# RG-LRU layer on one core: half-angle root, convolution split as a step of its own, weights split one block ahead, input gate's product beside the gates

## The chip, the cores and the metric

The kernel runs on one core of a Trainium2 chip. The metric is the device time of one execution in microseconds (us). Five engines work side by side, each through its own queue in order: TensorE (PE, with its weight loads as PEld), VectorE (DVE), ScalarE (ACT), GpSimd (POOL) and SyncE (SP), which here issues all DMA transfers.

## The reference

One inference step of two layers over 128 context tokens and 1024 latent tokens, 1024 channels each. The first layer (gated linear recurrence and neighbourhood attention) is not touched. The second layer is this:

```python
def odd_mixer(h, w_in, w_out, conv_w, conv_b, gate_w, gate_b, lam, s0):
    xb, g = jnp.split(h @ w_in, 2, axis=-1)
    xc = centred_dwconv(xb, conv_w, conv_b).astype(jnp.float32)
    ...
    for d in range(2):
        gates = jnp.einsum('bthi,ghij->gbthj', xblk, gate_w[d]...) + gate_b[d]
        r = jax.nn.sigmoid(gates[0])
        i = jax.nn.sigmoid(gates[1])
        log_a = -RG_C * r * jax.nn.softplus(-lam[d])
        a = jnp.exp(log_a)
        u = jnp.sqrt(-jnp.expm1(2.0 * log_a)) * (i * xc)
        hs, h_fin = linear_recurrence(a, u, s0[:, d])   # h[t] = a[t] * h[t-1] + u[t]; d = 1 runs backwards
    y = (outs[0] + outs[1]) * jax.nn.silu(g)
    return y @ w_out, ...
```

`RG_C` is 8, and the gate weights are eight blocks of 128 x 128 for each direction and gate. All of it is in float32.

## The kernel before

**Layout.** In the second layer channels lie on the 128 partitions and the 1152 tokens along the free dimension, in three chunks of 384. The eight groups of 128 channels are called j (0 to 7). float32 products on PE are made of three products: each operand is split into a rounded high half and the remainder, and high x high, high x low and low x high are summed in PSUM. The high half is an ACT copy (`wh`, `hTh`, `xch`, `yh`), the low half a subtraction on POOL or DVE (`wl`, `hTl`, `xcl`, `yl`).

**Input projection.** The 16 weight blocks of `w_in` are worked off in the order `ORD1` (0, 1, 2, 3, 8, 4, 9, 5, 10, 6, 11, 7, 12 to 15; blocks 0 to 7 give `xb` of one j, blocks 8 to 15 its gate path `g`), three units of 24 matmuls each (one per chunk), so 48 positions `pos`. `xb_unit` (L1143) writes its result from PSUM with ACT into the padded tile `xp`; `g_unit` (L1162) makes `sg` with ACT and DVE (L1171). Both begin with `w_get(i, 3, 3)`: load weight block i + 3 (tile `wraw`) and split up to i + 3 into `wh` and `wl` (L186).

**Per j, hung on positions.** `conv_all` (L1180) loads and splits the gate weights (`gw`) and runs `conv` (L1055): four DVE instructions over 1155 columns into `xc` (L1059, L1061), two ACT copies into `xch` and two DVE subtractions into `xcl` (L1067). `rg_front` (L1173) runs `gates` for both directions (per direction six groups of three matmuls into PSUM tags a and b, each taken out by an ACT tanh: the recurrence gate into `gr`, the input gate into `yT` or `gi`), then `rg_exp` twice: ACT tanh into `rt`, ACT exp in place in `gr`, which is then a; a squared into `ra` (on POOL for d = 0, L1112, on ACT for d = 1); and `rt = (a*a + 1) * rt` on DVE (L1113). `rg_root` is two ACT square roots, which need another function table than tanh and exp (L74 is the load of a table). `rg_back` runs `rg_scan` for both directions: input gate plus one times `xc` on DVE (four pieces, L1126), times the root on POOL (three chunks, L1128), the scan on DVE in four pieces (L1137), and for d = 1 the sum of both directions (L1142). `y_fin` multiplies by `sg` (L1177). The lists `PC`, `PF`, `PS`, `PK`, `PY` give the positions of convolution, front, root, back and end for each j.

**Output projection.** `w_split(.., V)` at the positions `WP` splits the eight blocks of `w_out`, with the low halves on DVE; `out_tiles` (L994 to L996) multiplies nine token tiles, the first two in an order that takes channel groups 6 and 7 last. `y_split` makes `yh` and `yl` (L977).

**What sets the order.** A scheduler turns the program into one queue for each engine. The order as written is a priority: an instruction whose inputs and buffers are ready by the scheduler's reckoning passes earlier ones that are not, and on the chip each queue then runs strictly in that order. Nearly all tiles of this layer wider than 512 columns, and the weights, come from one pool of 20 buffers (`slab`); a tile that finds none free waits for one, and so does the DMA that fills it. PSUM has three buffers of tag mm, one of o (both for the units) and two each of a and b.

Of the kernel before, what the change touches and what calls it, by code (L numbers as in the profile page):

```python
# [11 lines left out]
AF = mybir.ActivationFunctionType  # L12
OP = mybir.AluOpType
# [3 lines left out]
T = 1152  # L17
NCH = 3
CW = 384
# [14 lines left out]
def trunk_kernel(ctx: ExitStack, tc: tile.TileContext, x, wm0, wm, bmr, wfe, wv, woe, wfo, woo, rgw, sm, st0,  # L34
# [7 lines left out]
    V, A, G, PE = nc.vector, nc.scalar, nc.gpsimd, nc.tensor  # L42
# [4 lines left out]
    def slab(name, shape=(128, T), dt=F32):  # L47
        return sp.tile(list(shape), dt, name=name, tag="slab")
# [58 lines left out]
    def smc(n, i=None, j=None):  # L107
        a, b = SM[n]
        if i is None:
            return smt[:, a:b]  # L110
        return smt[:, a + i:a + (i + 1 if j is None else j)]
# [39 lines left out]
    V.tensor_scalar(sp_t[3], sp_t[3], 2.0, None, OP.mult)  # L151
    V.tensor_scalar(sp_t[0], sp_t[0], 0.0, None, OP.max)
    V.tensor_tensor(sp_t[3], sp_t[3], sp_t[0], OP.add)
    V.tensor_scalar(rgc, sp_t[3], 4.0, None, OP.mult)
    V.tensor_scalar(nrgc, sp_t[3], -4.0, None, OP.mult)
    V.tensor_scalar(hgb, smc("gateb"), 0.5, None, OP.mult)

# [38 lines left out]
    def w_get(i, la_load, la_split):  # L196
        w_split(i)
        w_split(i + la_split)
        w_load(i + la_load)
        return split[i]  # L200
# [845 lines left out]
        gw[h] = (hi, lo)  # L1046

    XP, XC, XS, GR, GI, RH = {}, {}, {}, {}, {}, {}

    def xc_of(j, a, b):  # L1050

        o = 0 if b <= 128 else 3
        return XC[j][:, a + o:b + o]

    def conv(j):  # L1055
        xp = XP.pop(j)
        acc = slab("xc", (128, 1155))
        w = [smc("convw", 4 * j + i) for i in range(4)]
        V.tensor_scalar(acc, xp[:, 0:1155], w[0], smc("convb", j), OP.mult, OP.add)  # L1059
        for i in (1, 2, 3):  # L1060
            V.scalar_tensor_tensor(acc, xp[:, i:i + 1155], w[i], acc, op0=OP.mult, op1=OP.add)  # L1061
        hi, lo = slab("xch", dt=F32R), slab("xcl", dt=F32R)
        XC[j], XS[j] = acc, (hi, lo)
        for a, b in ((0, 128), (128, T)):
            act(hi[:, a:b], xc_of(j, a, b), AF.Copy)
        for a, b in ((0, 128), (128, T)):
            V.tensor_tensor(lo[:, a:b], xc_of(j, a, b), hi[:, a:b].bitcast(F32), OP.subtract)  # L1067

    def gates(j, d):

        hi, lo = XS[j]
        wh, wl = gw[j]
        GR[j, d] = slab("gr")
        dst = [mini("yT") for c in range(3)] if d == 0 or j < 6 else None
        if d == 0:
            for c in range(3):
                yT[j, c] = dst[c]
        else:
            if dst is None:
                gi = slab("gi")  # L1080
                dst = [gi[:, c * CW:(c + 1) * CW] for c in range(3)]
            GI[j] = dst
        for c in range(3):
            z = slice(c * CW, (c + 1) * CW)
            for q in range(2):
                g = 2 * d + q
                ps = psum(("a", "b")[q])
                o = ps[:, :CW]
                n = slice(g * 128, (g + 1) * 128)
                PE.matmul(o, wh[:, n], hi[:, z], start=True, stop=False)  # L1090
                PE.matmul(o, wh[:, n], lo[:, z], start=False, stop=False)
                PE.matmul(o, wl[:, n], hi[:, z], start=False, stop=True)
                i = (d * 2 + q) * 8 + j
                act(GR[j, d][:, z] if q == 0 else dst[c], o, AF.Tanh, scale=0.5, bias=hgb[:, i:i + 1])
        if d == 1:
            XS.pop(j)
            gw.pop(j)

    RT = {}

    def rg_exp(j, d):

        r = GR[j, d]
        t = RT[j, d] = slab("rt")
        ci = slice(d * 8 + j, d * 8 + j + 1)
        act(t, r, AF.Tanh, scale=rgc[:, ci], bias=rgc[:, ci])
        act(r, r, AF.Exp, scale=nrgc[:, ci], bias=nrgc[:, ci])
        t2 = slab("ra")
        if d:
            act(t2, r, AF.Square)  # L1110
        else:
            G.tensor_tensor(t2, r, r, OP.mult)  # L1112
        V.scalar_tensor_tensor(t, t2, 1.0, t, op0=OP.add, op1=OP.mult)  # L1113

    def rg_sqrt(j, d):
        act(RT[j, d], RT[j, d], AF.Sqrt, scale=0.25)
# [1 line left out]
    def rg_scan(j, d):  # L1118
        a, r = GR.pop((j, d)), RT.pop((j, d))
        ci = d * 8 + j  # L1120
        s0c = smc("s0", ci)
        us = [yT[j, c] for c in range(3)] if d == 0 else GI.pop(j)
        segs = ((0, 0, 128), (0, 128, CW), (1, CW, 2 * CW), (2, 2 * CW, T))
        for c, x0, x1 in segs:
            u = us[c][:, x0 - c * CW:x1 - c * CW]
            V.scalar_tensor_tensor(u, u, 1.0, xc_of(j, x0, x1), op0=OP.add, op1=OP.mult)  # L1126
        for c in range(3):
            G.tensor_tensor(us[c], us[c], r[:, c * CW:(c + 1) * CW], OP.mult)  # L1128
        prev = {0: 0.0, 128: s0c} if d == 0 else {128: 0.0, T: s0c}
        for c, x0, x1 in segs[::-1] if d else segs:  # L1130
            u, av = us[c][:, x0 - c * CW:x1 - c * CW], a[:, x0:x1]
            st = prev.get(x1 if d else x0)
            if st is None:
                st = us[c + 1][:, 0:1] if d else us[c - 1][:, CW - 1:CW]
            if d:
                u, av = u[:, ::-1], av[:, ::-1]
            V.tensor_tensor_scan(u, av, u, st, OP.mult, OP.add)  # L1137
        V.tensor_copy(rgfin[:, ci:ci + 1], us[0][:, 0:1] if d else us[0][:, 127:128])
        if d:
            XC.pop(j)  # L1140
            for c in range(3):
                V.tensor_tensor(yT[j, c], yT[j, c], us[c], OP.add)  # L1142

# [2 lines left out]
    def xb_unit(j, c):  # L1146
        if j not in XP:
            XP[j] = slab("xp", (128, SLAB))
            V.memset(XP[j][:, 0:2], 0.0)
            V.memset(XP[j][:, 130:133], 0.0)  # L1150
            V.memset(XP[j][:, 1157:1158], 0.0)
        w_get(POS1[j], 3, 3)
        o = unit_f(POS1[j], c)
        if c == 0:
            act(XP[j][:, 2:130], o[:, 0:128], AF.Copy)
            act(XP[j][:, 133:389], o[:, 128:CW], AF.Copy)
        else:
            act(XP[j][:, 5 + c * CW:5 + (c + 1) * CW], o, AF.Copy)
        if c == 2:
            split.pop(POS1[j])  # L1160
# [1 line left out]
    SG = {}  # L1162

    def g_unit(j, c):
        w_get(POS1[8 + j], 3, 3)
        if j not in SG:
            SG[j] = slab("sg")
        o = unit_f(POS1[8 + j], c)
        sg = SG[j][:, c * CW:(c + 1) * CW]
        act(sg, o, AF.Tanh, scale=0.5)  # L1170
        V.scalar_tensor_tensor(sg, sg, 1.0, o, op0=OP.add, op1=OP.mult)  # L1171
        if c == 2:
            split.pop(POS1[8 + j])  # L1173
# [32 lines left out]
    ends = {n: i + 1 for i, (n, c) in enumerate(seq)}  # L1206
    ev = {}
    for j in range(8):
        for p, f in ((max(ends[j], PC[j]), conv_all), (PF[j], rg_front), (PS[j], rg_root), (max(PK[j], PS[j]), rg_back),
                     (max(PK[j] + 1, PS[j] + 1, ends[8 + j], PY[j]), y_fin)):  # L1210
            ev.setdefault(p, []).append((f, j))

# [5 lines left out]
    for pos in range(max(ev) + 1):  # L1218
# [6 lines left out]
        n, c = seq[pos]  # L1225
# [147 lines left out]
```

## Time and profile before

| | us |
|---|---|
| median of 3 runs (range) | 1283.1 (1281.62 to 1284.45) |
| the profiled execution | 1288.07 |
| its span, first to last instruction | 1286.1 |
| PE busy in the span | 1207.2 (94%) |
| DVE busy | 685.7 (53%) |
| ACT busy | 540.1 (42%) |
| POOL busy | 381.2 (30%) |

The profiled execution lies 5.0 us over the median, and 2.0 us of it lie outside the span. Matmuls are pipelined: one lasts about 340 ns in the records while they begin some 175 ns apart, so a busy PE says only that it wasn't standing. The second layer's mixer runs from about 904 us to 1184 us of the span, the output projection behind it until about 1280 us. A row of a timeline gives start, duration, engine, line, output and inputs, and in brackets how long the engine stood before it and what ended that.

### The profile page before, as it was taken

The page shows a single profiled execution, that of the slowest core. Times are in us where ns is not written, and L with a number is a line of the kernel's source. Part 1 is how long each engine was busy: PE and PEld are TensorE (multiplying, and loading weights), DVE is VectorE, ACT ScalarE, POOL GpSimd, SP SyncE. Part 2 cuts the span into 40 slices and gives each one's busy share as a digit, 9 for nine tenths or more (in the row PEclk, how much of TensorE's full clock was granted, in tenths as well). Part 3 has the DMA queues.
Part 4 walks back from the last instruction along what each step waited for, and adds up shares of the span by engine and source line. Part 5 has one row for each costly group of instructions (what it writes and reads, how often), then busy time and mean ns, then how long its engine had stood idle before and what let it go on. Part 6 is the DMA issues. An engine that isn't in the chain of part 4 may idle for free.

```text
span 1286.1 us, 19174 instructions
## 1 busy us (share of the span) xinstructions
PE 1207.2 (94%) x7536; PEld 1083.1 (84%) x7536; DVE 685.7 (53%) x1422; ACT 540.1 (42%) x1065; POOL 381.2 (30%) x271
## 2 busy tenths in 40 slices
PE   4999998999999999998999999999989899988997
PEld 3889998999999997887866667888988789987886
DVE  5547128315455200000267896644678978799844
ACT  3435134324342211111246774314467576676311
POOL 0143032420515110201250420117355564644000
PEclk8999999999998999998969999999989999999999
DMA  9410100111011455523320325223001101112432
GB/s 355 186 34 21 34 17 26 40 48 37 22 35 36 156 172 189 205 87 108 128 99 17 100 83 181 81 98 131 17 26 42 42 25 42 41 33 95 137 129 82
DMA packets 41909, 110.45 MB, mean 86 GB/s; under 512 B 4180, under 2 KB 14804, under 8 KB 41820
## 3 DMA queue, kind: packets, MB, share of 16 engines
q1 hardware_dynamic: 41820, 109.24, 25.2%
q8 instruction: 59, 0.97, 0.3%
q14 instruction: 30, 0.25, 0.1%
HBM read 96.61 MB, written 12.61 MB: 85 GB/s over the span
## 4 chain that ended last, share of the span: by engine, by line
PE 52%; DVE 14%; ACT 6%; issue 4%; DMA 4%; POOL 2%; SPq 1%; POOLq 0%; ACTq 0%; DVEq 0%
PE ps_mm L316 7%; PE ps_mm L318 7%; PE ps_mm L317 7%; PE ps_mm L995 5%; PE ps_mm L996 5%; PE ps_mm L994 5%; DMA wraw<-in_wfe_dram 3%; DVE yT L1137 2%; DVE xc L1061 2%; DVE P L857 2%; ACT P L77 1%; PE ps_a L221 1%; PE ps_mm L339 1%; PE ps_mm L341 1%; PE ps_mm L340 1%
## 5 line engine op out<-in xcount | busy, mean ns | idle before, releaser
L316 PE MATMUL ps_mm<-hTh,wh 128*128 128x384 f32 x936 | 321.2, 347 | 14.6 <-ACT xp L77 4.8
L317 PE MATMUL ps_mm<-hTl,wh 128*128 128x384 f32 x936 | 320.3, 343 | 2.3 <-DVE hTl L307 1.7
L318 PE MATMUL ps_mm<-hTh,wl 128*128 128x384 f32 x936 | 319.8, 342 | 1.1 <-POOL wl L186 1.1
L186 POOL TENSOR_TENSOR wl<-wraw,wh 128x1024 fp32r<-128x1024 f32 x50 | 127.5, 2552 | 284.3 <-ACT wh L77 254.6
L316 PEld LDWEIGHTS ps_mm<-hTh,wh 128*128 128x128 f32 x936 | 178.1, 191 | 31.1 <-ACT kq L77 7.4
L317 PEld LDWEIGHTS ps_mm<-hTl,wh 128*128 128x128 f32 x936 | 178.8, 191 | 4.6 <-DVE hTl L307 3.3
L318 PEld LDWEIGHTS ps_mm<-hTh,wl 128*128 128x128 f32 x936 | 178.7, 191 | 1.9 <-POOL wl L186 1.7
L995 PE MATMUL ps_mm<-wl,yh 128*128 128x512 f32 (+1 forms) x288 | 113.6, 395 | 4.6 <-DVE wl L186 4.6
L996 PE MATMUL ps_mm<-wh,yl 128*128 128x512 f32 (+1 forms) x288 | 112.6, 391 | 0.0
L994 PE MATMUL ps_mm<-wh,yh 128*128 128x512 f32 (+1 forms) x288 | 112.4, 392 | 0.0
L77 ACT ACTIVATE wh<-wraw 128x1024 fp32r<-128x1024 f32 x68 | 71.3, 1058 | 70.5 <-DMA wraw<-in_wfe_dram 40.6
L262 POOL TENSOR_TENSOR ss<-ss,nhalf 128x1 f32<-128x1 f32 x27 | 15.2, 564 | 243.4 <-DVE ss L261 186.2
L339 PE MATMUL ps_mm<-wh,hTh 128*128 128x256 f32 x288 | 83.2, 289 | 2.1 <-ACT va L77 2.1
L341 PE MATMUL ps_mm<-wh,hTl 128*128 128x256 f32 x288 | 82.0, 285 | 0.0
L340 PE MATMUL ps_mm<-wl,hTh 128*128 128x256 f32 x288 | 81.7, 284 | 0.0
L77 ACT ACTIVATE res<-xt 128x512 f32<-128x512 f32 (+1 forms) x37 | 23.0, 621 | 123.6 <-DVE xt L1004 115.7
L995 PEld LDWEIGHTS ps_mm<-wl,yh 128*128 128x128 f32 x288 | 54.5, 189 | 19.4 <-DVE wl L186 7.7
L822 POOL TENSOR_TENSOR nbm<-mkt,bT 128x384 f32<-128x384 f32 x42 | 45.5, 1103 | 85.2 <-DVE nm L868 40.4
L365 DVE SCALAR_TENSOR_TENSOR yT<-yT,ps_mm 128x384 f32<-128x384 f32 x10 | 5.5, 554 | 113.6 <-ACT yT L77 113.6
L994 PEld LDWEIGHTS ps_mm<-wh,yh 128*128 128x128 f32 x288 | 54.4, 189 | 12.3 <-issue 0.3
L996 PEld LDWEIGHTS ps_mm<-wh,yl 128*128 128x128 f32 x288 | 54.6, 189 | 11.4
L1128 POOL TENSOR_TENSOR yT<-yT,rt 128x384 f32<-128x384 f32 x42 | 56.4, 1371 | 23.4 <-ACT rt L77 19.3
(260 smaller groups left out, 2501.1 us busy)
## 6 DMA issues: line engine op xcount, KB each, us to landing
wm<-in_wm_dram SPq DMA_DIRECT2D x48, 512.0 KB
wraw<-in_wfe_dram SPq DMA_DIRECT2D x28, 512.0 KB
xt<-in_x_dram SPq DMA_DIRECT2D x18, 512.0 KB
bT<-in_bias_dram SPq DMA_DIRECT2D x48, 192.0 KB
wraw<-in_wfo_dram SPq DMA_DIRECT2D x16, 512.0 KB
x_d<-xt SPq DMA_DIRECT2D x9, 512.0 KB
xt<-x_d SPq DMA_DIRECT2D x9, 512.0 KB
out_dram<-xt SPq DMA_DIRECT2D x18, 256.0 KB
```

What stands on the lines that cost most here:

```text
L77: i = A.activation(out, in_, func, **kw)
L186: (lo_eng or G).tensor_tensor(lo, r, hi.bitcast(F32), OP.subtract)
L316: PE.matmul(o, w1, hh, start=(k == 0), stop=False)
L317: PE.matmul(o, w1, hl, start=False, stop=False)
L318: PE.matmul(o, w2, hh, start=False, stop=(k == 7))
L339: PE.matmul(o, hh, w1, start=(k == 0), stop=False)
L340: PE.matmul(o, hh, w2, start=False, stop=False)
L341: PE.matmul(o, hl, w1, start=False, stop=(k == 7))
L994: PE.matmul(o[:, :q - p], yh[:, z], wh[:, p:q], start=(k == 0), stop=False)
L995: PE.matmul(o[:, :q - p], yh[:, z], wl[:, p:q], start=False, stop=False)
L996: PE.matmul(o[:, :q - p], yl[:, z], wh[:, p:q], start=False, stop=(k == 7))
L1128: G.tensor_tensor(us[c], us[c], r[:, c * CW:(c + 1) * CW], OP.mult)
```

## The change

- `rg_exp` ends after tanh and exp. The constant `rgc` is halved, so the tanh is taken at half the angle; with x = -log a, tanh(x/2) = (1 - a)/(1 + a), and the square root of it times (1 + a) is the root of 1 - a*a. The factor is applied behind the root, by a DVE instruction at the head of `rg_scan`.
- The two ACT copies and two DVE subtractions of the split of `xc` leave `conv` for `conv_split`, hung two positions later.
- `w_get` in both units splits one block ahead; loads stay three ahead.
- The product (input gate + 1) * `xc` moves from `rg_scan` to the end of `gates`, and `xc` is given up there.

```diff
-    V.tensor_scalar(rgc, sp_t[3], 4.0, None, OP.mult)
+    V.tensor_scalar(rgc, sp_t[3], 2.0, None, OP.mult)
...
+        XC[j] = acc
+
+    def conv_split(j):
         hi, lo = slab("xch", dt=F32R), slab("xcl", dt=F32R)
-        XC[j], XS[j] = acc, (hi, lo)
+        XS[j] = (hi, lo)
...
+        for c, x0, x1 in SEGS:
+            u = dst[c][:, x0 - c * CW:x1 - c * CW]
+            V.scalar_tensor_tensor(u, u, 1.0, xc_of(j, x0, x1), op0=OP.add, op1=OP.mult)
         if d == 1:
             XS.pop(j)
+            XC.pop(j)
...
-        t2 = slab("ra")
-        if d:
-            act(t2, r, AF.Square)
-        else:
-            G.tensor_tensor(t2, r, r, OP.mult)
-        V.scalar_tensor_tensor(t, t2, 1.0, t, op0=OP.add, op1=OP.mult)
...
+        V.scalar_tensor_tensor(r, a, 1.0, r, op0=OP.add, op1=OP.mult)
         us = [yT[j, c] for c in range(3)] if d == 0 else GI.pop(j)
-        segs = ((0, 0, 128), (0, 128, CW), (1, CW, 2 * CW), (2, 2 * CW, T))
-        for c, x0, x1 in segs:
-            u = us[c][:, x0 - c * CW:x1 - c * CW]
-            V.scalar_tensor_tensor(u, u, 1.0, xc_of(j, x0, x1), op0=OP.add, op1=OP.mult)
...
-        w_get(POS1[j], 3, 3)
+        w_get(POS1[j], 3, 1)
...
-        w_get(POS1[8 + j], 3, 3)
+        w_get(POS1[8 + j], 3, 1)
...
-        for p, f in ((max(ends[j], PC[j]), conv_all), (PF[j], rg_front), ...
+        for p, f in ((max(ends[j], PC[j]), conv_all), (max(ends[j], PC[j]) + 2, conv_split), (PF[j], rg_front), ...
```

## Rows read from the trace of the kernel before

**Rows 1.** The page's slices (40 equal ones; busy share of TensorE in tenths).
```profile
PE   4999998999999999998999999999989899988997
```
**Rows 2.** Waits of PE, 860 us on, for DVE: total us, times, longest.
```profile
PE ps_mm L995 <- DVE wl L186: 4.1, 4, 2.0
```
**Rows 3.** Timeline of PE: the five matmuls that ended its long waits for ACT.
```profile
958.08 0.69 PE L316 MATMUL ps_mm<-hTh,wh 128*128 128x384 f32 x1 [4.79 <-ACT xp L77]
...
994.46 0.45 PE L1090 MATMUL ps_a<-xch,gw 128*128 128x384 f32 x1 [2.03 <-ACT gr L77]
...
1026.43 0.69 PE L1090 MATMUL ps_b<-xch,gw 128*128 128x384 f32 x1 [6.16 <-ACT yT L77]
...
1061.25 0.45 PE L1090 MATMUL ps_a<-xch,gw 128*128 128x384 f32 x1 [3.22 <-ACT gr L77]
...
1130.63 0.69 PE L1090 MATMUL ps_a<-xch,gw 128*128 128x384 f32 x1 [3.51 <-ACT gr L77]
```
**Rows 4.** Stretches: length, busy us (instructions) of PE, PEld, DVE, ACT, POOL, PEclk.
```profile
956.20:962.80 6.60, 4.72 (x15) 4.72 (x16) 6.60 (x16) 4.83 (x10) 2.45 (x1) 0.50 0.01 2
963.00:969.80 6.80, 6.80 (x39) 6.45 (x39) 5.49 (x9) 4.86 (x7) 0.70 (x2) 1.00 0.26 77
...
904.00:1184.00 280.00, 254.75 (x1378) 246.01 (x1376) 230.65 (x300) 191.29 (x270) 143.53 (x81) 0.96 0.13 40
```
**Rows 5.** Timeline of ACT: two of the copies `xch` and their waits.
```profile
956.33 1.26 ACT L77 ACTIVATE xch<-xc 128x128 fp32r<-128x128 f32 x2 [5.05 <-DVE xc L1061]
...
1023.45 1.26 ACT L77 ACTIVATE xch<-xc 128x128 fp32r<-128x128 f32 x2 [11.32 <-DVE xc L1061]
```
**Rows 6.** Waits of DVE and of ACT, 904 to 1190 us.
```profile
DVE rt L1113 <- POOL ra L1112: 23.5, 6, 9.4
...
ACT xch L77 <- DVE xc L1061: 38.5, 7, 11.3
```
**Rows 7.** Timeline of DVE: L1113 and what came ahead of the convolutions.
```profile
940.46 1.36 DVE L1113 SCALAR_TENSOR_TENSOR rt<-ra,rt 128x1152 f32<-128x1152 f32 x1 [9.39 <-POOL ra L1112]
943.39 1.36 DVE L1113 SCALAR_TENSOR_TENSOR rt<-ra,rt 128x1152 f32<-128x1152 f32 x1 [1.56 <-ACT ra L77]
944.66 1.59 DVE L1059 TENSOR_SCALAR xc<-xp,smt 128x1155 f32<-128x1155 f32 x1
...
971.69 1.36 DVE L1113 SCALAR_TENSOR_TENSOR rt<-ra,rt 128x1152 f32<-128x1152 f32 x1 [3.20 <-POOL ra L1112]
...
1004.11 4.86 DVE L1113 SCALAR_TENSOR_TENSOR rt<-ra,rt 128x1152 f32<-128x1152 f32 x2 [2.00 <-POOL ra L1112]
...
1039.97 1.36 DVE L1113 SCALAR_TENSOR_TENSOR rt<-ra,rt 128x1152 f32<-128x1152 f32 x1 [4.88 <-POOL ra L1112]
```
**Rows 8.** Group of POOL, 904 to 1190 us: busy us, mean ns, idle.
```profile
L1112 POOL TENSOR_TENSOR ra<-gr 128x1152 f32<-128x1152 f32 x8 | 25.4, 3175 | 52.9 <-ACT gr L77 42.0 <-DMA wraw<-in_wfo_dram 6.5 <-issue 4.3
```
**Rows 9.** Group of DVE, the input gate's product, 904 to 1190 us.
```profile
L1126 DVE SCALAR_TENSOR_TENSOR yT<-yT,xc 128x384 f32<-128x384 f32 (+2 forms) x56 | 23.6, 473 | 1.7 <-ACT yT L77 1.7
```
**Rows 10.** Waits of the DMA queue for buffers, 860 to 1200 us.
```profile
SPq L56 <- PE ps_a L1092: 90.5, 5, 22.0
```
**Rows 11.** POOL: low halves of weight block 5, and of 14 and 15.
```profile
931.19 2.41 POOL L186 TENSOR_TENSOR wl<-wraw,wh 128x1024 fp32r<-128x1024 f32 x1 [9.29 <-ACT wh L77]
...
1107.83 4.91 POOL L186 TENSOR_TENSOR wl<-wraw,wh 128x1024 fp32r<-128x1024 f32 x2 [2.73 <-ACT wh L77]
```
**Rows 12.** PE: first matmuls of weight blocks 2 (two joined) and 12.
```profile
911.12 0.51 PE L316 MATMUL ps_mm<-hTh,wh 128*128 128x384 f32 x2
...
1103.64 0.44 PE L316 MATMUL ps_mm<-hTh,wh 128*128 128x384 f32 x1 [2.00 <-DVE sg L1171]
```
**Rows 13.** A split of `w_out` on DVE; last `yl` of chunk 0, its use.
```profile
1173.96 1.22 DVE L186 TENSOR_TENSOR wl<-wraw,wh 128x1024 fp32r<-128x1024 f32 x1
...
1195.84 1.02 DVE L977 TENSOR_TENSOR yl<-yT,yh 128x384 fp32r<-128x384 f32 x2
...
1196.31 0.39 PE L994 MATMUL ps_mm<-wh,yh 128*128 128x512 f32 x1
```

More of the change, by code (lines that the diff above doesn't have):

```diff
@@ L1048, in trunk_kernel @@
     XP, XC, XS, GR, GI, RH = {}, {}, {}, {}, {}, {}
+    SEGS = ((0, 0, 128), (0, 128, CW), (1, CW, 2 * CW), (2, 2 * CW, T))
     def xc_of(j, a, b):
@@ L1129, in rg_scan @@
         prev = {0: 0.0, 128: s0c} if d == 0 else {128: 0.0, T: s0c}
-        for c, x0, x1 in segs[::-1] if d else segs:
+        for c, x0, x1 in SEGS[::-1] if d else SEGS:
             u, av = us[c][:, x0 - c * CW:x1 - c * CW], a[:, x0:x1]
@@ L1139, in rg_scan @@
         if d:
-            XC.pop(j)
             for c in range(3):
@@ L1208, in trunk_kernel @@
     for j in range(8):
-        for p, f in ((max(ends[j], PC[j]), conv_all), (PF[j], rg_front), (PS[j], rg_root), (max(PK[j], PS[j]), rg_back),
+        for p, f in ((max(ends[j], PC[j]), conv_all), (max(ends[j], PC[j]) + 2, conv_split), (PF[j], rg_front), (PS[j], rg_root), (max(PK[j], PS[j]), rg_back),
                      (max(PK[j] + 1, PS[j] + 1, ends[8 + j], PY[j]), y_fin)):
```

## Prediction, made before the changed kernel was run

> **What bounds the kernel now.** First the slices of the page [rows 1]: PE is at 9 tenths or more nearly everywhere, so in the changed layer only the time in which PE stands, or runs at the lower clock, can be won. Next the waits of PE in the layer: five long ones for ACT, 4.79, 2.03, 6.16, 3.22 and 3.51 us, 19.7 us together [rows 3], and 4.1 us for low halves of `w_out` that DVE makes late [rows 2]. Then the clock: behind the first of them the granted clock is 0.50, the 1.2 GHz level, and 15 matmuls are busy 4.72 us (315 ns each); in the stretch behind it, at 1.00, 39 take 6.80 us (174 ns) [rows 4]. I put that at 2.2 us lost behind each of the two longest waits (4.8 us of matmuls at 1.2 GHz, 45% of it) and 1.5 us behind each of the last two, with half as long a stretch; the 2.03 us wait has none. The five waits with their slow stretches are 19.7 + 7.4 = 27.1 us.
>
> Why is ACT late? Its timeline shows it standing in front of `xch`, 5.05 us and 11.32 us in the two rows shown [rows 5], 38.5 us in seven such waits [rows 6], for the convolution on DVE. Units and gates that PE has finished wait in PSUM behind that copy, until PE has no buffer left. And why is DVE late? Over the same stretch it stood 23.5 us in front of L1113 for the square `ra` from POOL [rows 6]; the convolution came right behind L1113 [rows 7]. Between 904 and 1184 us DVE is busy for 230.65 of 280 us [rows 4], so time that it stands is not easily made up. That is the chain on which the forecast rests: POOL's square, DVE's L1113, the convolution, ACT's `xch`, PE.
>
> **The change part by part.** The sum is made against the profiled execution, 1288.07 us with a span of 1286.1; the median lies 5.0 us lower, and I take the same difference for the changed kernel.
>
> *Half-angle root.* It removes eight POOL squares (25.4 us [rows 8]) and eight on ACT, and L1113 from its place; neither POOL nor ACT bounds the layer, so their work is worth nothing by itself. What counts is DVE's standing ahead of a convolution: 9.39 + 1.56 us ahead of the one whose `xch` held PE for 4.79 us, 3.20 us ahead of the next (2.03), 2.00 us ahead of the third (6.16), 4.88 us ahead of the fourth (3.22) [rows 3, 7]; none ahead of the fifth (3.51). Where the removed wait is longer than the stall, the stall goes with its slow stretch: 4.79 + 2.2, 2.03, 3.22 + 1.5; of the third 2.00 us. Together 15.7 us. What is late next is DVE's own work (the scans that stand between the four convolution instructions).
>
> The multiplication comes back as one DVE instruction for each direction, ahead of POOL's products. In the middle of the layer the back step has positions to spare; at j = 7 it lies on the path: the last `yl` of chunk 0 is made from 1195.84 on, its matmuls begin at 1196.31 [rows 13], no margin. Alone L1113 takes 1.36 us; the two rows at 1004.11 take 4.86 us together, 1.36 and about 3.5 beside a POOL product [rows 7]. Bounds: -6 (the root no longer waits for POOL and DVE, and comes earlier) to +7; I take +1.4, one uncovered instruction, since the second runs beside POOL's products of the first direction.
>
> At this point a rule speaks against the change. The rows show it first: the second of those two instructions became 2.1 us longer while POOL worked. The Trainium skill, "SBUF — State Buffer", section "Who interferes with whom", says that a DVE instruction with both inputs in SBUF contends with a GpSimd instruction that reads SBUF. By that rule all 16 moved multiplications, which now stand next to POOL's products, would lengthen by as much: 34 us of DVE time as an estimate from the row. I don't add it: only what delays a convolution or the end reaches PE, and the bounds above hold that part; but it is the reason for not counting POOL's 25.4 us as relief.
>
> *Convolution's split two positions later.* Nothing is added. By priority two units' results (2 x 24 x 174 ns = 8.4 us of PE) now pass ahead of `xch`. The scheduler may still put it where it was, since it goes by readiness; so the bounds are 0 and what is left of the third and fifth stall, 4.16 + 2.2 + 3.51 + 1.5 = 11.4 us. I take 4.2, the rest of the third, where units stood behind the copy; behind the fifth stood gate results, which the position doesn't move.
>
> *Weights split one block ahead.* Per block the same ACT copy and POOL subtraction, later, on the queues that they are on now; the loads keep their place. In 11 blocks (5 to 15) the low half ended on average 23.6 us behind the first matmul of the block at which it was asked for: 22.5 us for the first (911.12 to 933.60), 9.1 for the last (1103.64 to 1112.74) [rows 11, 12]. Blocks follow each other every 19.3 us ((1103.64 - 911.12)/10 [rows 12]). Three blocks of lead hid that; one wouldn't, if the delay stayed. Much of it, though, is the load's wait for a buffer (90.5 us of such waits for one releaser alone [rows 10]), and the load is now two blocks ahead of the split; the subtraction itself is about 2.4 us [rows 11]. And with two blocks held raw instead of split, four buffers become two, the two `ra` go, and waits for buffers shrink. Bounds 0 and +50 (11 x 4.6); I take +3, two late blocks of 1.5 us.
>
> *`w_out`.* Blocks 60 and 61 were split by `w_get` on POOL; asked for later, they fall to `WP`'s call with DVE as the engine: two more DVE subtractions ahead of the first output matmuls, which already wait 4.1 us for DVE [rows 2]. At 1.22 us each [rows 13], +2.4; bounds 0 and +5 (both stretched beside POOL as the one at 1004.11 was [rows 7]).
>
> *Input gate's product.* The same DVE instructions (23.6 us for the 56 into `yT` [rows 9]), asked for earlier. They waited only 1.7 us in all for their inputs [rows 9], so they already ran right behind the gates, and the position of `gates` of j still lies behind the convolution of j + 1: nothing, bounds -2 (`xc` is freed earlier) and +3 (one j's pieces ahead of a convolution).
>
> **Sum:** -15.7 - 4.2 + 1.4 + 3 + 2.4 = -13.1 us: 1275.0 for a profiled execution, **1270.0 us** for the median.
>
> **The rivals.** *All stalls go* (chance 0.10): the five waits with their slow stretches and half of the costs: -27.1 + 3.4, and some 4 of the waits for `w_out`, so -28: 1255. For it: buffers are the layer's scarcest good [rows 10], and this frees four; against: no margin at the end [rows 13] and a DVE that is busy for 82% [rows 4].
>
> *Only the removed waits count* (0.10): the scheduler leaves `xch` where it was; the sum without the 4.2: 1274.
>
> *The wait moves* (0.12): DVE now stands in front of the new multiplication for the root from ACT, where the next convolution is again queued behind it, and half of the 15.7 and all of the 4.2 are gone; costs 6.8 against 7.9: 1282, no difference.
>
> *Weights become the bound, slower* (0.20): the low half of a block ends behind the block's first matmul. It decides from the point at which a split takes longer than the 19.3 us between blocks, and the mean delay so far is 23.6. If five of the 11 blocks are late by 4.6 us, each with a slow stretch of 1.5 us, that is +30 against the -20 won and the other costs of 3.8: +14, but part of it would fall where PE stands now; between 1287 and 1297, I take 1293. For it: ACT stood for up to 11.32 us in front of one copy [rows 5], and a split queued behind it is late by as much. Against: the load is done two blocks earlier.
>
> **How the numbers follow.** The forecast itself has 0.48 (1262 to 1278 by its terms). With 0.10 each for all and for only the removed waits, faster by over 0.2% (2.6 us, about what a measurement of this kernel can tell from no change) has 0.68, within 0.2% 0.12, slower 0.20. The range goes from 1252, below the all-gone case, to 1290, which takes in the milder half of the slower case: some 0.14 are left out above and below.
>
> **What would show it.** Right: no wait of DVE for POOL ahead of a convolution; ACT's waits in front of `xch` well under 38.5 us; PE's waits for ACT under 8 us in place of 19.7, and one or two slow stretches in the layer fewer. The weights' rival shows as PE waits at L316 or L318 for `wh` or `wl`; the moved wait as DVE standing at the head of `rg_scan` for ACT's root; the end as PE waiting at L995 or L996 for DVE. The forecast is wrong if the five stalls stay although DVE no longer waits for POOL: then the convolution was late for another reason, the scans or buffers.

## The result, and the profile after

The changed kernel takes 1277.86 us (median of 19 runs, 1274.01 to 1284.33), the kernel before, measured beside it, 1284.45 us (19 runs). The ratio is 0.9938 with a 95% interval of 0.9922 to 0.9954: faster by 0.6%, or 8.0 us (the two medians lie 6.6 us apart). The forecast was 1270.0 us, 13.1 less than before, so the direction came true and the time lies in the range, but only some three fifths of the gain came. The profiled execution has 1281.0 us and a span of 1279.2 (before 1288.07 and 1286.1).

In the changed kernel the convolution is L1060 and L1062, the low halves `xcl` L1071, the gates' matmuls L1094 to L1096, the input gate's product L1101, the new multiplication L1124, POOL's product L1127, the scan L1136, `sg` L1169.

To see where the time went I cut the span at two places of the timeline: the start of the first convolution, and the start of the last matmul of the input projection. What lies between them is called the mixer here, the rest up to the span's end the tail. Before, the mixer takes 259.0 us and the tail 114.2; after, 247.6 and 119.4. The layer won 11.4 us and gave 5.2 back.

The waits of PE from 904 us on in the changed kernel (total us, times, longest):

```profile
PE ps_mm L994 <- ACT yh L77: 5.8, 1, 5.8
PE ps_a L1094 <- ACT gr L77: 4.4, 2, 4.2
PE ps_mm L316 <- DVE sg L1169: 3.6, 2, 3.3
PE ps_b L1094 <- ACT yT L77: 3.5, 1, 3.5
PE ps_o L318 <- POOL wl L186: 1.8, 1, 1.8
PE ps_mm L996 <- DVE yl L977: 1.7, 1, 1.7
PE ps_mm L995 <- DVE wl L186: 1.5, 2, 0.8
```

L994 to L996 are the output projection: 9.3 us of waits in the tail (with 0.3 for a `wh`), where there were 4.1 [rows 2]. The others lie in the mixer: 13.3 us in place of 21.8. Of the five waits for ACT [rows 3] three are gone, two (4.2 and 3.5 us) remain, and there are new ones for `sg` and for one late low half of a weight block. With them a stretch at the lower clock is gone: the windows show three of them with 13.7 us in all, before there were four with some 20.6 (the first is [rows 4]). Columns are those of [rows 4]:

```profile
949.90:956.70 6.80, 6.57 (x22) 6.58 (x23) 6.80 (x10) 4.89 (x10) 5.28 (x3) 0.53 0.00 0
987.40:990.90 3.50, 3.32 (x12) 3.33 (x13) 3.50 (x8) 3.50 (x7) 0.00 (x0) 0.57 0.31 64
1100.10:1103.50 3.40, 3.40 (x13) 3.40 (x13) 1.94 (x2) 0.63 (x1) 1.30 (x1) 0.57 0.18 67
```

At a little over half the rate 6.9 us less of such time gives some 3 us; with 8.5 us less waiting that makes up the mixer's 11.4.

The waits of ACT (904 to 1160 us) and of DVE (904 to 1190 us):

```profile
ACT xch L77 <- DVE xc L1062: 10.1, 3, 4.8
...
DVE yT L1136 <- POOL yT L1127: 11.9, 10, 3.3
DVE rt L1124 <- ACT rt L77: 5.6, 3, 2.2
```

DVE no longer waits for a square, and `xch` stands 10.1 us behind the convolution in place of 38.5 [rows 6]. What DVE has instead is 11.9 us of waits at the scan for POOL's product (3.8 before), and 5.6 us at the new multiplication.

### The profile page after: what moved, and what is told of

Read it like the earlier page. It is cut to its first block, busy times and chain, and to the rows that moved or that the text cites. A ratio compares the mean times of both kernels' runs of the same rounds, so it can differ in the third digit from the quotient of the medians.

```text
span 1279.2 us, 19143 instructions
## 1 busy us (share of the span) xinstructions
PE 1204.3 (94%) x7536; PEld 1082.4 (85%) x7536; DVE 680.5 (53%) x1424; ACT 529.2 (41%) x1057; POOL 349.1 (27%) x261
## 5 line engine op out<-in xcount | busy, mean ns | idle before, releaser
L316 PE MATMUL ps_mm<-hTh,wh 128*128 128x384 f32 x936 | 320.1, 346 | 11.2 <-DVE yT L365 4.2
L186 POOL TENSOR_TENSOR wl<-wraw,wh 128x1024 fp32r<-128x1024 f32 x48 | 123.5, 2574 | 285.9 <-ACT wh L77 251.1
L994 PE MATMUL ps_mm<-wh,yh 128*128 128x512 f32 (+1 forms) x288 | 112.8, 393 | 6.1 <-ACT yh L77 5.8
L996 PE MATMUL ps_mm<-wh,yl 128*128 128x512 f32 (+1 forms) x288 | 112.5, 391 | 1.7 <-DVE yl L977 1.7
L1127 POOL TENSOR_TENSOR yT<-yT,rt 128x384 f32<-128x384 f32 x42 | 56.8, 1382 | 72.2 <-DVE rt L1124 72.2
L77 ACT ACTIVATE res<-xt 128x512 f32<-128x512 f32 (+1 forms) x37 | 22.9, 619 | 124.9 <-DVE xt L1004 117.0
L994 PEld LDWEIGHTS ps_mm<-wh,yh 128*128 128x128 f32 x288 | 54.6, 190 | 18.6 <-ACT yh L77 6.3
L996 PEld LDWEIGHTS ps_mm<-wh,yl 128*128 128x128 f32 x288 | 54.5, 189 | 13.7 <-DVE yl L977 2.3
```

The source lines that it names most:

```text
L77: i = A.activation(out, in_, func, **kw)
L186: (lo_eng or G).tensor_tensor(lo, r, hi.bitcast(F32), OP.subtract)
L316: PE.matmul(o, w1, hh, start=(k == 0), stop=False)
L994: PE.matmul(o[:, :q - p], yh[:, z], wh[:, p:q], start=(k == 0), stop=False)
L996: PE.matmul(o[:, :q - p], yl[:, z], wh[:, p:q], start=False, stop=(k == 7))
```

## The experiments

Every run below is one kernel with its expectation as it stood beforehand. This table puts the runs side by side. "PE stood" is the sum of PE's waits in that part; the sum of mixer and tail leaves the first layer out, whose length differs by several us between executions; the ratio is that of the timed runs to the kernel before.

| kernel | root | split step | weights ahead | product moved | buffers | mixer us (PE stood) | tail us (PE stood) | sum against before | ratio, 95% |
|---|---|---|---|---|---|---|---|---|---|
| before | | | 3 | | 20 | 259.0 (21.8) | 114.2 (4.1) | | 1 |
| e1_half | new | | 3 | | 20 | 262.7 (24.9) | 118.4 (7.6) | +7.9 | 1.0028 (0.9998 to 1.0058) |
| e2_split | | new | 3 | | 20 | 262.6 (29.1) | 116.9 (5.0) | +6.3 | 1.0038 (1.0004 to 1.0072) |
| e3_look | | | 1 | | 20 | 259.5 (21.9) | 117.1 (5.8) | +3.4 | 1.0006 (0.9971 to 1.0041) |
| e4_prod | | | 3 | yes | 20 | 259.5 (21.3) | 113.7 (3.9) | 0.0 | 0.9975 (0.9944 to 1.0007) |
| after | new | new | 1 | yes | 20 | 247.6 (13.3) | 119.4 (9.3) | -6.2 | 0.9938 (0.9922 to 0.9954) |
| m1_half | | new | 1 | yes | 20 | 259.5 (22.2) | 112.9 (3.9) | -0.8 | 0.9991 (0.9965 to 1.0017) |
| m2_split | new | | 1 | yes | 20 | 246.7 (13.3) | 118.5 (7.5) | -8.0 | 0.9954 (0.9917 to 0.9991) |
| m3_look | new | new | 3 | yes | 20 | 259.8 (22.9) | 116.2 (6.3) | +2.8 | 1.0027 (1.0006 to 1.0049) |
| m4_prod | new | new | 1 | | 20 | 248.9 (13.6) | 120.1 (9.4) | -4.2 | 0.9956 (0.9938 to 0.9974) |
| n1_half_look | new | | 1 | | 20 | 250.3 (14.2) | 118.8 (7.6) | -4.1 | 0.9966 (0.9941 to 0.9991) |
| s1_look3_b21 | new | new | 3 | yes | 21 | 249.7 (16.0) | 115.1 (4.6) | -8.4 | 0.9928 (0.9906 to 0.9950) |
| t1_root45 | new, early | new | 1 | yes | 20 | 246.0 (11.7) | 127.5 (16.8) | +0.3 | 1.0005 (0.9981 to 1.0029) |
| s2_after_b21 | new | new | 1 | yes | 21 | 242.7 (11.1) | 119.3 (9.0) | -11.2 | 0.9910 (0.9877 to 0.9944) |

### One edit alone

**The half-angle root on the kernel before.**

```diff
-    V.tensor_scalar(rgc, sp_t[3], 4.0, None, OP.mult)
+    V.tensor_scalar(rgc, sp_t[3], 2.0, None, OP.mult)
...
-        t2 = slab("ra")
...
-        V.scalar_tensor_tensor(t, t2, 1.0, t, op0=OP.add, op1=OP.mult)
...
+        V.scalar_tensor_tensor(r, a, 1.0, r, op0=OP.add, op1=OP.mult)
```

> The kernel before with the half-angle root alone (no squares; the multiplication by 1 + a behind the root). Theory A, the gain comes from DVE no longer standing for POOL's square: DVE's 23.5 us of waits at L1113 go, PE's waits for ACT in the mixer fall from 19.7 us to under 10, and the time falls by 4 to 8 us, most of the change's gain. Theory B, the gain comes from freed buffers, above all those of the weights: within 3 us of before. Theory C, any edit shuffles the scheduler's order: a change of some us with no link to the waits at L1113.

Measured: 1.0028. ACT's waits for the convolution did fall, from 38.5 to 20.8 us, and yet PE stood 24.9 us in place of 21.8. The timelines of ACT and PE in this kernel show one of its stalls:

```profile
1016.93 1.06 ACT L77 ACTIVATE wh<-wraw 128x1024 fp32r<-128x1024 f32 x1 [7.50 <-POOL yT L1123]
...
1021.26 0.58 ACT L77 ACTIVATE gr<-ps_a,hgb 128x384 f32<-128x384 f32 x1 [2.90 <-DVE yT L1172]
...
1021.89 0.69 PE L1090 MATMUL ps_a<-xch,gw 128*128 128x384 f32 x1 [8.17 <-ACT gr L77]
```

ACT copies `wh` from `wraw`, which comes by DMA; POOL's product into `yT` (L1123) is no input of it. What that product does is read `rt` for the last time, and so free a slab. ACT stood 7.50 us for a buffer to write to, with the gates that PE had finished queued behind. So I sorted ACT's waits from 904 to 1160 us by the releaser: one that makes the input (PE's results, a DMA, `xc` for `xch`), or another one, which I read as a buffer coming free. The second kind is 5.0 us before, 30.4 us here, and 20.6 us in the changed kernel, which is the faster one: the sum alone doesn't give the time. That sorting is mine: it goes by the names in the rows.

**The convolution's split alone.**

```diff
+        XC[j] = acc
+
+    def conv_split(j):
...
+        ... (max(ends[j], PC[j]) + 2, conv_split), ...
```

> The kernel before with the convolution's split as a step two positions later, alone. Theory A: ACT takes unit results ahead of xch, its waits in front of xch fall from 38.5 us to under 25, and the time falls by 2 to 5 us; DVE's waits for the square stay near 23 us. Theory B: no difference within 2 us, since no buffer is freed. Theory C: some us either way.

Measured: 1.0038, PE's waits 29.1 us, almost all for `gr`, and ACT's waits for buffers 27.8 us. Alone it costs time.

**The shorter lead alone.**

```diff
-        w_get(POS1[j], 3, 3)
+        w_get(POS1[j], 3, 1)
...
-        w_get(POS1[8 + j], 3, 3)
+        w_get(POS1[8 + j], 3, 1)
```

> The kernel before with weights split one block ahead instead of three, alone. Theory A: no gain; PE waits for low halves of weights (L318) appear, 2 to 5 us, time from 0 to 5 us longer. Theory B: two blocks held raw free two buffers, waits of the loads for buffers fall, the time falls by 5 us or more.

Measured: 1.0006, no difference that shows; PE stood 21.9 us, 3.7 of it for late low halves of weights.

**The product alone.**

```diff
+        for c, x0, x1 in SEGS:
+            u = dst[c][:, x0 - c * CW:x1 - c * CW]
+            V.scalar_tensor_tensor(u, u, 1.0, xc_of(j, x0, x1), op0=OP.add, op1=OP.mult)
```

> The kernel before with the input gate's product at the end of gates, alone (the convolution's result is given up there too). Theory A: within 2 us of before, since the product ran right behind the gates already. Theory B: 2 to 4 us faster by the buffer of the convolution's result. Theory C: some us either way.

Measured: 0.9975, with an interval that takes in 1; the mixer and PE's waits are those of before. No single edit gains anything that these runs can tell from nothing, and the four ratios together would make the kernel slower (+0.5%). The gain is in a combination.

### One edit taken out

Each of these is the changed kernel with one of the four diffs above put back.

> The changed kernel with the squares and the whole angle restored, the other three edits kept. None of the four edits alone made the kernel faster, so they work together or not at all. Theory A2 (the half-angle root is the basis; the other edits let its gain through): the gain goes, ratio to before 0.998 to 1.005, DVE's waits for POOL's square return (15 us or more). Theory B2 (the three order edits carry the gain, the root nothing): ratio 0.993 to 0.996. Theory C (chance of the order): anything, with no link to those waits.

Squares restored: 0.9991, and the mixer is back at 259.5 us with 22.2 us of waits. The root is needed.

> The changed kernel with the convolution's split put back into the convolution, the other three edits kept. Theory A2: ACT stands in front of xch again, over 20 us in place of 10.1, PE's waits for ACT in the mixer rise by 4 us or more, ratio to before 0.996 to 1.0. Theory B2: the same if this edit is one that carries the gain. If the edit does nothing: ratio 0.992 to 0.996.

Split put back into the convolution: 0.9954, mixer 246.7 us. ACT's waits for `xc` are 19.7 us in place of 10.1, but PE stood 13.3 us in all either way, in other places. The split step is not needed.

> The changed kernel with weights split three blocks ahead again, the other three edits kept. Theory A2: little difference or a gain, PE's 2.4 us of waits for POOL's low halves go, ratio 0.991 to 0.996. Theory B2 (buffers): loads and convolutions wait longer for buffers, PE's waits for ACT grow, ratio 0.997 to 1.003.

Three blocks ahead again: 1.0027, mixer 259.8 us. Here ACT's waits for the convolution are the shortest of all (8.1 us), and PE stood as long as before. ACT's waits for buffers are 36.9 us. The first rows are from ACT's list of waits, the others from the timelines of POOL, ACT and PE:

```profile
ACT xch L77 <- DVE xc L1062: 8.1, 2, 4.8
ACT xch L77 <- POOL wl L186: 8.0, 1, 8.0
ACT gw L77 <- DVE yT L1136: 6.9, 1, 6.9
...
979.05 2.34 POOL L186 TENSOR_TENSOR wl<-wraw,wh 128x1024 fp32r<-128x1024 f32 x1
...
981.42 1.26 ACT L77 ACTIVATE xch<-xc 128x128 fp32r<-128x128 f32 x2 [8.01 <-POOL wl L186]
...
984.72 0.69 PE L1094 MATMUL ps_a<-xch,gw 128*128 128x384 f32 x1 [8.85 <-ACT gr L77]
```

The copy `xch`, whose input had been ready since 972.3 us, stood 8.01 us until POOL had made the low half of a weight block and so given up its raw block; 3.3 us later PE ends a wait of 8.85 us.

> The changed kernel with the input gate's product put back into the back step, the other three edits kept. Theory A2: within 2 us of the changed kernel, ratio 0.992 to 0.997. Theory C (chance of the order): a difference of 4 us or more for an edit that removes no work and no wait.

Product put back: 0.9956, in an interval that overlaps that of the changed kernel, and mixer 248.9 us: not needed.

So the root and the shorter lead are needed, both of them, and one theory explains it: the root takes away a wait for inputs, then ACT and POOL reach the limit of the pool of 20 slabs, and a block that is split three ahead holds two slabs (high and low half) where a raw one holds one. Its rivals are that the two edits need the others after all, and that the lead matters by the order of the queues and not by buffers.

### The pair, and one buffer more

> The kernel before with two of the four edits: half-angle root and weights split one block ahead. Theory P (the pair carries the gain: the root removes the wait for inputs, the shorter lead gives back the slab buffers that ACT would then stand for): ratio to before 0.993 to 0.996, like the full change, ACT's waits for the convolution's xc under 22 us in the mixer, its waits for a free buffer under 25, PE's waits for ACT's gr and yT buffers under 12. Rival A (each edit adds its own small part, by the single-edit runs 1.0028 and 1.0006): 1.003, no gain. Rival S (the split step is needed as third): between, 0.998 or above, with ACT's waits for xc as in the root alone (20.8).

The kernel before with the diffs of root and lead: 0.9966, a little over the range expected of the pair; mixer 250.3 us, PE stood 14.2 us. The pair brings 8.7 of the mixer's 11.4 us; in the timed runs 4.4 of 8.0 us, and their intervals overlap. ACT's waits for buffers are 6.3 us. Its own price shows too: 4.5 us of waits for low halves of weights.

```profile
PE ps_a L1090 <- ACT gr L77: 8.8, 4, 3.0
...
PE ps_mm L318 <- POOL wl L186: 3.4, 2, 2.1
PE ps_o L318 <- POOL wl L186: 1.1, 1, 1.1
```

**A 21st slab with three blocks ahead.** This is m3_look with one buffer more and nothing else; three constants of the first layer, each with room of its own, now share one slab that comes free.

```diff
-    sp = ctx.enter_context(tc.tile_pool(name="slabs", bufs=20))
+    sp = ctx.enter_context(tc.tile_pool(name="slabs", bufs=21))
...
-    am = const.tile([128, 256], I32, name="am")
+    lay1 = slab("lay1", (128, 1024))
+    am = lay1[:, 768:1024].bitcast(I32)
```

> The changed kernel with the weights split three blocks ahead again (that alone gave 1.0027), but with 21 slab buffers in the second layer in place of 20: three constants of the first layer share one slab. Theory B (what one block ahead gives is free slab buffers): one buffer more gives back half of what two gave, ratio to before 0.998 to 1.000, ACT's waits for a free buffer well under the 36.9 us of the run with 20, and PE's waits for the gates' result buffer gr under half of 21.6. Rival O (what one block ahead gives is order: the split no longer stands ahead of other work on ACT and POOL): 1.002 to 1.004, as with 20 buffers, and ACT's waits for buffers stay above 30.

Measured: 0.9928, against 1.0027 with 20, in intervals that lie apart. One buffer is worth about 1% here, as much as the shorter lead (1.0027 to 0.9938), and more than was expected of it. The rows below are PE's and ACT's waits: `gr` holds PE for 11.7 us in place of 21.6 (a little over the half that was expected), and the 7.3 us wait of `xch` for a raw block is still there. Of the five stalls for `gr` in m3_look the first two stayed (2.73 and 8.85 us there, 2.80 and 7.02 here), one shrank from 5.69 to 1.90 us and two of some 2 us went. ACT's waits for buffers are 26.4 us, not half of 36.9: that sum is a sign of the shortage and no measure of what it costs; only those waits count that have PE's results queued behind them.

```profile
PE ps_a L1095 <- ACT gr L77: 11.7, 3, 7.0
...
ACT xch L77 <- POOL wl L187: 7.3, 1, 7.3
```

The lead's own place in the queues falls as the cause with this run: the lead is three here. But the scheduler reckons with free buffers, so the 21st also changes the order of the queues: in the mixer some 20 of DVE's 286 instructions and some 10 of ACT's 250 stand elsewhere than in m3_look, the first of them about 60 us behind the first convolution. This pair alone doesn't separate the buffer from the order that comes with it. The Trainium skill, "Perfetto Trace Analysis", section "Identifying Performance Opportunities", says that gaps which come back for a stretch on the engine that should be full can mean a shortage of SBUF or PSUM for the next tile. This pair of runs agrees: five waits for `gr` with 21.6 us, then three with 11.7, by one tile.

### The tail

In the changed kernel PE waits 5.8 us for the last unit's `yh` (channel group j = 7). The timelines of ACT, DVE, POOL and PE, in order of time (POOL's row is the first of three products):

```profile
1166.22 1.28 ACT L74 ACT_TABLE_LOAD   x1
...
1168.48 2.21 ACT L77 ACTIVATE rt<-rt 128x1152 f32<-128x1152 f32 x2
...
1169.66 2.63 DVE L1124 SCALAR_TENSOR_TENSOR rt<-gr,rt 128x1152 f32<-128x1152 f32 x2 [2.11 <-ACT rt L77]
1171.17 2.00 POOL L1127 TENSOR_TENSOR yT<-yT,rt 128x384 f32<-128x384 f32 x1 [27.02 <-DVE rt L1124]
1175.16 2.03 DVE L186 TENSOR_TENSOR wl<-wraw,wh 128x1024 fp32r<-128x1024 f32 x1 [2.86 <-POOL yT L1127]
1177.11 1.24 DVE L1136 TENSOR_TENSOR_SCAN yT<-gr,yT 128x128 f32<-128x128 f32 x1
...
1186.88 0.80 PE L994 MATMUL ps_mm<-wh,yh 128*128 128x512 f32 x1 [5.82 <-ACT yh L77]
```

The root begins 8.7 us behind the mixer's end (1159.8). From it to the first scan 8.6 us pass: the new multiplication, POOL's product, and a `wl` that stands in DVE's queue ahead of the scan and waits 2.86 us, as I read it, for the buffer that the last of three products frees. In the kernel before the same distance is 2.3 us:

```profile
1177.84 1.17 ACT L77 ACTIVATE rt<-rt 128x1152 f32<-128x1152 f32 x1
...
1180.14 1.22 DVE L1137 TENSOR_TENSOR_SCAN yT<-gr,yT 128x128 f32<-128x128 f32 x1 [0.83 <-POOL yT L1128]
```

The distance goes with the root and with the buffers: it is 8.6 us in all six kernels with the new root at this position and 20 slabs, 4.7 and 4.8 us in the two with 21, and 2.2 to 2.4 us in the five with the squares. I tried the other end: the root earlier.

```diff
-    PS = [11, 17, 22, 26, 32, 38, 42, 51]
+    PS = [11, 17, 22, 26, 32, 38, 42, 45]
```

> The changed kernel with the last unit's root (j = 7) placed at position 45 in place of 51, ahead of the last gate units. Theory T (PE's wait of 5.8 us for yh and the slow stretch behind it come from the root's late table load, 12 us behind the gates that feed it): the wait goes or falls under 2 us, ratio to the kernel before 0.988 to 0.992 (4 to 7 us below the changed kernel). Rival G (the extra table load and the root ahead of the last sg copies hold PE's PSUM, or DVE and POOL set the end): 0.993 to 0.996, with the wait moved to sg or yT, or yh waiting still 4 us or more.

Measured: 1.0005, the gain is gone. The wait for `yh` did go, and two longer ones came, as PE's waits show:

```profile
PE ps_mm L994 <- DVE sg L1169: 9.0, 1, 9.0
PE ps_mm L996 <- DVE yl L977: 7.8, 1, 7.8
```

The mixer is as short as ever (246.0 us), the tail is 127.5. DVE now has the scans of j = 7 in its queue ahead of the last `sg`: its `sg` instructions, which free PSUM, begin at 1161.84, while PE had stood since 1153.4. So the late root protects the end of the input projection, as far as this one earlier position shows. The rival's mechanism was right, and its price too low by half a per cent. A position between 45 and 51 wasn't tried.

### The best of both

> The changed kernel (weights split one block ahead) with 21 slab buffers in the second layer in place of 20, three constants of the first layer sharing one slab. Theory B (free slab buffers are still what is short with one block ahead): ACT's waits for a free buffer in the mixer fall from 20.6 us to under 15, PE's waits there from 12.8 us to under 8, ratio to before 0.987 to 0.991, below both the changed kernel (0.9938) and the one with three blocks ahead and 21 buffers (0.9928). Rival E (buffers are no longer short once two are given back; what is left is DVE's scans and the last unit's root): 0.992 to 0.995, PE's waits in the mixer above 10 us, and its wait for yh still 4 us or more.

The changed kernel with the diff of the 21st slab: 0.9910, median 1272.48 us (6 runs), the shortest mixer (242.7 us) and the lowest middle value of all kernels here; its interval (0.9877 to 0.9944) overlaps that of the changed kernel. It lies at the border of the two expectations: PE still stood 11.1 us in the mixer, more than the 8 of theory B and above the 10 of its rival, and ACT's waits for buffers fell only to 16.4 us. By ratio it is the one, by waits the other: with the lead already short, the buffer brings less than it does with three blocks ahead (0.3% in place of 1%). The wait for `yh` is gone from the tail, but `yl` of the same group holds PE instead. The three rows are PE's waits:

```profile
PE ps_mm L997 <- DVE yl L978: 8.6, 2, 6.9
PE ps_a L1095 <- ACT gr L77: 4.1, 1, 4.1
PE ps_mm L317 <- DVE sg L1170: 3.7, 2, 3.4
```

This run does separate the buffer from the order. In the mixer ACT, POOL and PE work off the same instructions in the same order as in the changed kernel, by the names in the rows, and DVE does so up to 179 us behind the first convolution. The changed kernel's second stall lies ahead of that (75 us). There ACT stands in front of `rt`, a slab, until POOL's product has given one up, with the gates' result `yT` queued behind. The timelines of ACT and PE, first the changed kernel, then s2_after_b21:

```profile
985.71 1.35 ACT L77 ACTIVATE rt<-gr,rgc 128x1152 f32<-128x1152 f32 x1 [2.78 <-POOL yT L1127]
...
987.58 0.69 PE L1094 MATMUL ps_b<-xch,gw 128*128 128x384 f32 x1 [3.45 <-ACT yT L77]
...
973.68 1.35 ACT L77 ACTIVATE rt<-gr,rgc 128x1152 f32<-128x1152 f32 x1 [1.03 <-POOL yT L1128]
...
975.54 0.44 PE L1095 MATMUL ps_b<-xch,gw 128*128 128x384 f32 x1 [1.09 <-ACT yT L77]
```

One slab more, and the stall falls from 3.45 to 1.09 us. So one of the two waits for ACT that the changed kernel kept is a wait for a buffer.

## Why the prediction was half right

**The chain was read rightly.** POOL's square, DVE's L1113, the convolution, `xch`, PE: with the squares gone DVE waits for POOL at that place no more, and the waits of `xch` fell to 10.1 us. PE's waits for ACT in the mixer are 7.9 us (4.4 and 3.5), just under the 8 that was named, and one slow stretch went. With the waits for `yh` and `wh` in the tail they are 14.0 us, and the first sign, that DVE waits for POOL no more ahead of a convolution, was not met at one place, told next.

**Root, -15.7: too large.** Given the other three edits it is worth 11.9 us of mixer (m1_half to after). The step that failed is that the first stall goes with its slow stretch. It stayed, 4.16 us in place of 4.79, and the timelines of DVE, POOL, ACT and PE tell why:

```profile
938.04 1.36 DVE L1124 SCALAR_TENSOR_TENSOR rt<-gr,rt 128x1152 f32<-128x1152 f32 x1
...
940.52 3.52 POOL L186 TENSOR_TENSOR wl<-wraw,wh 128x1024 fp32r<-128x1024 f32 x1
944.00 3.04 POOL L1127 TENSOR_TENSOR yT<-yT,rt 128x384 f32<-128x384 f32 x3
...
945.04 1.22 DVE L1136 TENSOR_TENSOR_SCAN yT<-gr,yT 128x128 f32<-128x128 f32 x1 [3.26 <-POOL yT L1127]
946.17 2.08 DVE L1062 SCALAR_TENSOR_TENSOR xc<-xp,smt,xc 128x1155 f32<-128x1155 f32 x1
...
948.35 1.26 ACT L77 ACTIVATE xch<-xc 128x128 fp32r<-128x128 f32 x2 [4.82 <-DVE xc L1062]
...
950.13 0.69 PE L1094 MATMUL ps_a<-xch,gw 128*128 128x384 f32 x1 [4.16 <-ACT gr L77]
```

DVE stands 3.26 us at a scan for POOL's product, and the convolution's last instruction is behind that scan in the queue. That is the rival in which the wait moves, with another place than I gave it: not at the head of `rg_scan`, where DVE stood 5.6 us in all, but one step on. The new multiplication is not what the product waited for: it had ended at 939.40, and the product began at 944.00, behind the gate weights' low half (from 938.06 on) and a `wl` in POOL's queue. The four kernels with root, split step and short lead (after, m4_prod, t1_root45, s2_after_b21) all have this stall, with 4.1 to 4.2 us; in the two with root and lead but without the split step (m2_split, n1_half_look) PE stands 2.1 us at the same matmul, for a late `wl`. So in the changed kernel the stall hangs on the order that comes with the split step; why the scheduler puts the `wl` ahead there isn't shown. The moved wait took the first stall and none of the others.

**What the term left out** is larger than its error: that the removed waits turn into waits for buffers. Alone the root gave nothing (1.0028). I had priced the buffers with the lead, as something that shrinks, and not with the root, which needs them.

**The split step, -4.2: nothing.** The third stall went also without it (m2_split has the same sum of waits, 13.3 us, and none longer than 2.7). Putting ACT's copy behind two units halves the copy's waits, but units weren't what PE lacked.

**The lead, +3: the sign was wrong for this kernel.** Its cost is what I took it for, one late block of 1.8 us in the changed kernel and 4.5 us in the pair alone. But without it the mixer is 12.2 us longer (m3_look). The rival in which weights become the bound has the right place and a price that is several times too high: the splits ended 23.6 us behind the point at which they were asked for while nobody waited for them, and asked for later they came sooner (9.5 us behind that point on average in the changed kernel, counted the same way). A delay of work that nobody waits for is no measure of the shortest it could have.

**The tail, +1.4 and +2.4: +5.2 in all, in other shares.** PE's waits for `w_out`'s low halves fell from 4.1 to 1.5 us, so that term has the wrong sign; the two extra splits lie at 1156 to 1162 us, ahead of the last unit's root. The root's part was to be one uncovered instruction; it is 6.3 us more between root and first scan. The multiplication is some 1.3 us of that, as counted. The rest I had not seen, above all the `wl` that slips in ahead of the scan. POOL's first of three products ends at 1173.17, where the scan could have begun; it began at 1177.11. With a 21st slab the distance is 3.8 us shorter, which speaks for the buffer as what that `wl` waits for. The distance isn't all of the tail, though: counted from the mixer's end, the root begins 2.8 us later than before (8.7 and 5.9 us), and from the first scan to `yh` it takes 5.0 us less (9.2 and 14.2), so that `yh` comes 4.1 us later. All of the tail's 5.2 us are PE's waits, 9.3 against 4.1. That no margin was left there [rows 13] was right.

**The product, 0:** as predicted (e4_prod, m4_prod).

**The sum.** Mixer -11.4 in place of -16.9 (root, split step and lead together), tail +5.2 in place of +3.8, and 0.7 us less in the first layer: the 6.9 us by which the spans differ. That the time lay in the range is in part luck. The prediction counted the root without the buffers that it needs and the lead as a cost, and these two errors go opposite ways: by its terms the change without the lead would have been at least 16.1 us faster, and measured it is no faster at all (m3_look, 1.0027). And 1277.86 us lies at the edge of the forecast's own band, between two rivals (1274 and 1282), so that the time by itself confirms none of them.

**The rule on the shared port.** Of the sixteen moved multiplications only one is clearly longer than L1113's median before (1358 ns), the 2176 ns below. The changed kernel's rows for the line give shortest, median and longest in ns, and behind it the convolution:

```profile
L1124 DVE SCALAR_TENSOR_TENSOR rt<-gr,rt x16: 1324/1351/2176, 938.0 to 1170.9; 128x1152 f32<-128x1152 f32 x16
...
L1062 DVE SCALAR_TENSOR_TENSOR xc<-xp,smt,xc x24: 1410/1422/3491, 913.1 to 1107.1; 128x1155 f32<-128x1155 f32 x24
```

So leaving the 34 us out was right, though not because the two engines never meet. Nine of the sixteen meet no work of POOL. Of the other seven, six run for 1.1 to 1.3 us beside it and still take 1346 to 1356 ns. There POOL pays: its product beside the multiplication took 2.00 us at 1171.17, and the next one, alone, 1.01. The row from which I took the 34 us was also misread: the instruction of 3.5 us at 1004.11 ran beside a `wl` on POOL (1004.69 to 1007.75), not beside a product. The Trainium skill, "SBUF — State Buffer", section "Who interferes with whom", has a DVE instruction with two SBUF inputs contend with a GpSimd instruction that reads SBUF. The convolution agrees: the sixteen of its 24 instructions that meet no work of POOL take 1.41 to 1.43 us, and all that take more than 1.5 us (up to 3.49) run beside a `wl` or a product. In the five profiles with the squares the 24 have means of 1699 to 1891 ns, in the nine without them 1488 to 1700 ns. The squares themselves are not what lengthens them: of those 120 convolution instructions two ran beside a square, with 1.39 and 1.41 us.

**What stays open:** why the split step alone costs 0.4%; how much of the 1% of the 21st buffer at a lead of three comes by the order of the queues; whether the 21st buffer adds anything to the changed kernel, whose intervals overlap; and a place for the last root, or for the multiplication behind it, that costs the tail nothing.

## What to carry to other kernels

When a wait for data is taken away, ask how many buffers the freed engines may now fill: if the pool is full, the same engine stands again, now in front of an instruction whose inputs are all there, and the trace names a releaser that has nothing to do with its data. An edit that only holds less (a shorter lead, one constant less in SBUF) can be the needed half of another, so single-edit runs alone would have thrown both away. At the end of a layer count the whole chain from the moved instruction to the first user, and what slips into the queue while it waits.

## What was unexpected of the hardware

One slab more (1152 columns of float32) changed the time by about 1% (1.0027 to 0.9928), with the layer's work left as it was. And POOL's elementwise work and DVE's showed in each other's times even when neither waits for the other's result: the same convolution instruction took 1.41 us at its shortest and 3.49 us, beside POOL, at its longest in one execution, and POOL's product 2.00 us beside DVE's multiplication in place of 1.01.
